# A hardware loop over the middle tiles on VectorE, and waits moved to other engines

## The chip, the core and the metric

The kernel runs on one core of a Trainium2 chip. Five engines work side by side, each through its own list of instructions: TensorE, VectorE, ScalarE, GpSimd (POOL) and SyncE (SP). They meet through semaphores, which are counters that an instruction can raise, lower or wait for. Sixteen DMA engines move data between the chip's large memory (DRAM) and the on-chip memory of 128 partitions. The metric is the time of one execution on the device, in microseconds; given is the median of ten runs.

## What is computed

The input is a float32 array of 8 x 64 x 256 x 256. In each plane of 256 x 256, every 8 x 8 window has its own maximum subtracted from it. The output has the size of the input.

```python
def reference(x):
    B, C, H, W = x.shape
    pH, pW = 8, 8
    oH, oW = H // pH, W // pW
    x_r = x.reshape(B, C, oH, pH, oW, pW)
    pooled = x_r.max(axis=(3, 5))
    upsampled = np.repeat(np.repeat(pooled, pH, axis=2), pW, axis=3)
    return (x - upsampled).astype(np.float32)
```

Input and output are 134.2 MB each. Every byte is read once and written once.

## The kernel before

Eight lines of a plane, 2,048 values, form a "row": it holds 32 whole windows. There are 16,384 rows, 128 for each of 128 partitions. A tile is 4 rows in each partition, so 512 rows or 4 MB, and there are 32 tiles. Six tile buffers (slots) lie on the chip, and tile i uses slot i mod 6. The subtraction works in place, so a slot holds a tile from its load until its store has landed.

Nothing schedules this kernel. It is written for four hands, and each engine takes its own instructions in the order of the loop over the tiles in line 46:

- SyncE issues the loads (L62). Before it loads into a used slot, it waits until the slot's last store has landed (L57, semaphore `stored[slot]`). DMAs raise their semaphore by 16.
- VectorE waits for the load (L75), takes the maximum of each window with one reduce for the whole tile (L76), waits until that reduce has written its result (L87, semaphore `reduced`), and subtracts, with one instruction for each row (L89). The last subtraction raises `ready` (L95).
- ScalarE waits for `ready` (L97) and issues the store (L98). It computes nothing.
- TensorE and GpSimd have no part in it.

The waits of lines 75 and 87 don't become instructions of their own: each is carried by the reduce or the subtraction after it. The semaphore values grow through the kernel, so each of the 32 tiles has its own instructions, with its own numbers in them. VectorE's list has 174 instructions.

Two tiles are cut finer (line 11). The first is loaded in two DMAs of 2 rows and stored in two. The last is loaded whole, and reduced, subtracted and stored in pieces of 2, 1 and 1 rows. At the end SyncE waits for the stores of all six slots (L103).

Of the kernel before, what the change touches and what calls it, by code (L numbers as in the profile page):

```python
# [1 line left out]

# [4 lines left out]

F32 = mybir.dt.float32
ROW = 2048

TILES = [([2, 2], [2, 2])] + [([4], [4])] * 30 + [([4], [2, 1, 1])]
SLOTS = 6
LOAD_SEMS = 10


@with_exitstack
def kernel(
    ctx: ExitStack,
    tc: tile.TileContext,
    x: bass.AP,  # L20
    out: bass.AP,
):
    nc = tc.nc
    P = nc.NUM_PARTITIONS
    B, C, H, W = x.shape
    pH = pW = 8
    oW = W // pW

    x_rows = x.rearrange("b c (oh ph) w -> (b c oh) (ph w)", ph=pH)
    out_rows = out.rearrange("b c (oh ph) w -> (b c oh) (ph w)", ph=pH)  # L30
    assert sum(sum(loads) for loads, _ in TILES) * P == x_rows.shape[0]
    size = max(sum(loads) for loads, _ in TILES)

    data = ctx.enter_context(tc.tile_pool(name="data", bufs=1))
    dats = [data.tile([P, size * ROW], F32, name=f"dat{i}") for i in range(SLOTS)]
    tops = [data.tile([P, size * oW], F32, name=f"tops{i}") for i in range(SLOTS)]
    loaded = [tc.alloc_semaphore(f"loaded{i}") for i in range(LOAD_SEMS)]
    stored = [tc.alloc_semaphore(f"stored{i}") for i in range(SLOTS)]
    reduced = tc.alloc_semaphore("reduced")
    ready = tc.alloc_semaphore("ready")  # L40

    with tc.tile_critical(no_gpsimd_drain=True):  # L42
        at = 0
        n_loads = n_reduced = n_ready = 0
        n_stored = [0] * SLOTS
        for i, (loads, stores) in enumerate(TILES):
            slot = i % SLOTS
            dat, top = dats[slot], tops[slot]

            rows = sum(loads)  # L50
            src = x_rows[at : at + P * rows].rearrange("(p r) d -> p (r d)", r=rows)
            dst = out_rows[at : at + P * rows].rearrange("(p r) d -> p (r d)", r=rows)
            at += P * rows


            if n_stored[slot]:
                nc.sync.wait_ge(stored[slot], 16 * n_stored[slot])  # L57
            lo = 0
            ends = {}
            for R in loads:  # L60
                part = slice(lo * ROW, (lo + R) * ROW)
                nc.sync.dma_start(out=dat[:, part], in_=src[:, part]).then_inc(  # L62
                    loaded[n_loads % LOAD_SEMS], 16
                )
                ends[lo] = (loaded[n_loads % LOAD_SEMS], 16 * (n_loads // LOAD_SEMS + 1))
                n_loads += 1
                lo += R

            lo = 0
            for R in stores:  # L70
                part = slice(lo * ROW, (lo + R) * ROW)
                wins = dat[:, part].rearrange("p (r ph ow pw) -> p r ph ow pw", r=R, ph=pH, ow=oW)
                maxs = top[:, lo * oW : (lo + R) * oW].rearrange("p (r ow) -> p r ow", r=R)
                if lo in ends:
                    nc.vector.wait_ge(*ends[lo])  # L75
                nc.vector.tensor_reduce(  # L76
                    out=maxs if R > 1 else maxs[:, 0],
                    in_=(
                        wins.rearrange("p r ph ow pw -> p r ow ph pw")
                        if R > 1  # L80
                        else wins[:, 0].rearrange("p ph ow pw -> p ow ph pw")
                    ),
                    axis=mybir.AxisListType.XY,
                    op=mybir.AluOpType.max,
                ).then_inc(reduced, 1)
                n_reduced += 1
                nc.vector.wait_ge(reduced, n_reduced)  # L87
                for r in range(R):
                    sub = nc.vector.tensor_tensor(  # L89
                        out=wins[:, r],  # L90
                        in0=wins[:, r],
                        in1=maxs[:, r].unsqueeze(1).unsqueeze(3).to_broadcast([P, pH, oW, pW]),
                        op=mybir.AluOpType.subtract,
                    )
                sub.then_inc(ready, 1)  # L95
                n_ready += 1
                nc.scalar.wait_ge(ready, n_ready)  # L97
                nc.scalar.dma_start(out=dst[:, part], in_=dat[:, part]).then_inc(stored[slot], 16)  # L98
                n_stored[slot] += 1
                lo += R  # L100

        for slot in range(SLOTS):
            nc.sync.wait_ge(stored[slot], 16 * n_stored[slot])  # L103


# [1 line left out]
_INS = ['x']  # L107
_OUTS = [((8, 64, 256, 256), 'float32')]


# [23 lines left out]
```

## Time and profile before

| | |
|---|---|
| median of 10 runs | 627.85 us (627.73 to 628.08) |
| the profiled execution | 627.9 us |
| its span, from the first to the last instruction of the program | 626.1 us |
| one reduce of a whole tile, 30 times | 8.685 us |
| one subtraction of one row, 128 times | 2.286 us |
| load of 4 MB, issue to landing (median) | 62.5 us |
| store of 4 MB, issue to landing (median) | 36.0 us |

The span is what the trace covers; 1.8 us of the execution lie around it. Busy time counts only instructions that compute. The time from issue to landing contains the time in which a transfer stands behind others in its queue: a load of 4 MB has mostly other loads in front of it.

The queues of the trace are called q1 (the loads that SyncE issues), q10 (the stores that ScalarE issues) and q14 (instructions[...]). All of them share the 16 DMA engines.

### The profile page before, as it was taken

The numbers are of one execution on the slowest core, as the hardware profiler recorded it, in microseconds if no ns is written. First come the engines' busy times: TensorE is split into PE (matmuls) and PEld (weight loads), VectorE is DVE, ScalarE is ACT, GpSimd is POOL, SyncE is SP. The second block draws the span as 40 slices with busy tenths as digits, with TensorE's granted clock in tenths as the row PEclk, the third lists the DMA queues.
The fourth block names the chain that finished last, engine by engine and source line by source line (L and its number), as shares of the span: only waits on it lengthen the run. The fifth ranks groups of instructions, "written<-read, shape, count | busy, mean of one in ns | idle before, by whom it ended". The sixth has DMA issues, their size and how long they took to land.

```text
span 626.1 us, 286 instructions
## 1 busy us (share of the span) xinstructions
DVE 562.6 (90%) x163; POOL 0.2 (0%) x4
## 2 busy tenths in 40 slices
DVE  4999999998898888988889888899888998888983
POOL 0000000000000000000000000000000000000000
DMA  8999999999999999999999999999999999999998
GB/s 368 402 431 440 435 435 435 431 433 427 430 431 427 435 435 435 433 435 435 435 435 435 435 429 433 425 435 427 431 435 435 433 435 435 435 435 435 435 429 343
DMA packets 9793, 268.45 MB, mean 429 GB/s; under 512 B 1088, under 2 KB 1088, under 8 KB 1088
## 3 DMA queue, kind: packets, MB, share of 16 engines
q1 hardware_dynamic: 4752, 134.22, 49.9%
q10 hardware_dynamic: 5040, 134.22, 49.7%
q14 instruction: 1, 0.01, 0.0%
HBM read 134.22 MB, written 134.22 MB: 429 GB/s over the span
## 4 chain that ended last, share of the span: by engine, by line
DVE 90%; another core or an unknown queue 7%; DMA 1%; issue 0%; SPq 0%
DVE dat L89 46%; DVE tops L76 44%; DMA dat<-in_x_dram 1%; SPq L129 0%; SPq L42 0%
## 5 line engine op out<-in xcount | busy, mean ns | idle before, releaser
L76 DVE TENSOR_REDUCE tops<-dat 128x128 f32<-128x8192 f32 (+2 forms) x35 | 278.3, 7953 | 52.3 <-DMA dat<-in_x_dram 52.3
L89 DVE TENSOR_TENSOR dat<-dat,tops 128x2048 f32<-128x2048 f32 x128 | 285.0, 2286 | 1.2
L118 POOL MEMSET const-bfloat16-1.0<- 128x1 bf16 x1 | 0.1, 102 | 0.0
L118 POOL MEMSET const-uint8-127<- 128x1 uint8 x1 | 0.1, 102 | 0.0
L118 POOL MEMSET const-float32-0.0<- 128x1 f32 x1 | 0.1, 99 | 0.2 <-issue 0.2
L118 POOL MEMSET const-float32-1.0<- 128x1 f32 x1 | 0.1, 99 | 0.0
## 6 DMA issues: line engine op xcount, KB each, us to landing
dat<-in_x_dram SPq DMA_DIRECT2D x31, 4096.0 KB, 62.5
out_dram<-dat ACTq DMA_DIRECT2D x30, 4096.0 KB, 36.0
out_dram<-dat ACTq DMA_DIRECT2D x3, 2048.0 KB, 19.6
dat<-in_x_dram SPq DMA_DIRECT2D x2, 2048.0 KB, 9.7
out_dram<-dat ACTq DMA_DIRECT2D x2, 1024.0 KB, 9.7
```

Of the source, the lines that this page charges most:

```text
L76: nc.vector.tensor_reduce(out=maxs if R > 1 else maxs[:, 0], in_=(wins.rearrange("p r ph ow pw -> p r ow ph pw") if R > 1 else wins[:, 0]. ...
L89: sub = nc.vector.tensor_tensor(out=wins[:, r], in0=wins[:, r], in1=maxs[:, r].unsqueeze(1).unsqueeze(3).to_broadcast([P, pH, oW, pW]), op ...
L118: nc = _bacc.Bacc("TRN2", target_bir_lowering=False, num_devices=1)
```

## The change

The work on the data is the same: the same tiles, the same reduces and subtractions, one load and one store for each middle tile. What differs is how it is put to the engines.

- VectorE's thirty middle tiles are a loop that the engine itself runs: five turns of an outer loop, six of an inner one over the slots, with one tile as the body (after, L139 to L146). Its list has 55 instructions, 17 of them in the inner loop. Addresses in the body are worked out from the loop's counter, by register instructions in front of the reduce and of the second, third and fourth subtraction.
- Since the body is the same for each tile, it can't wait for growing values. VectorE waits for 1 and lowers the semaphore by 1 (`take`, L73). These waits are instructions of their own, for `reduced` as for the loads.
- Loads raise one semaphore for each slot. TensorE waits for them in the order of the tiles and raises one common semaphore, `filled`, by 1 for each (L116 to L120). VectorE takes from `filled`.
- The six slots are one buffer, `ring`, and the results of the reduces one buffer, `tops`. Tile 0 uses slot 5, tile 1 slot 0, and so on.
- The first tile is loaded, worked on and stored in pieces of 1, 1 and 2 rows. The last is as before.
- The stores of the last six tiles raise one semaphore, `final`, and ScalarE waits for it behind its last store (L133). SyncE has no wait at the end.

```diff
-TILES = [([2, 2], [2, 2])] + [([4], [4])] * 30 + [([4], [2, 1, 1])]
+HEAD = [1, 1, 2]
+SIZE = 4
+ROUNDS = 5
+TAIL = [2, 1, 1]
 SLOTS = 6
-LOAD_SEMS = 10
...
-    dats = [data.tile([P, size * ROW], F32, name=f"dat{i}") for i in range(SLOTS)]
-    tops = [data.tile([P, size * oW], F32, name=f"tops{i}") for i in range(SLOTS)]
-    loaded = [tc.alloc_semaphore(f"loaded{i}") for i in range(LOAD_SEMS)]
+    ring = data.tile([P, SLOTS * SIZE * ROW], F32, name="ring")
+    tops = data.tile([P, SLOTS * SIZE * oW], F32, name="tops")
+    first = [tc.alloc_semaphore(f"first{i}") for i in range(len(HEAD))]
+    loaded = [tc.alloc_semaphore(f"loaded{i}") for i in range(SLOTS)]
     stored = [tc.alloc_semaphore(f"stored{i}") for i in range(SLOTS)]
+    final = tc.alloc_semaphore("final")
+    filled = tc.alloc_semaphore("filled")
     reduced = tc.alloc_semaphore("reduced")
     ready = tc.alloc_semaphore("ready")
...
+    def take(sem, n):
+        nc.vector.wait_ge(sem, n).then_inc(sem, -n)
+
+    def pool_and_subtract(part, top, R):
+        wins = part.rearrange("p (r ph ow pw) -> p r ph ow pw", r=R, ph=pH, ow=oW)
+        maxs = top.rearrange("p (r ow) -> p r ow", r=R)
+        nc.vector.tensor_reduce(
...
+        ).then_inc(reduced, 1)
+        take(reduced, 1)
+        for r in range(R):
+            sub = nc.vector.tensor_tensor(
...
+            )
+        sub.then_inc(ready, 1)
...
+        landed = [0] * SLOTS
+        for i in range(len(sizes)):
+            slot = slot_of(i)
+            if landed[slot]:
+                nc.sync.wait_ge(stored[slot], 16 * landed[slot])
+            for k, (lo, R) in enumerate(cuts(HEAD if i == 0 else [sizes[i]])):
+                part = slice(lo * ROW, (lo + R) * ROW)
+                nc.sync.dma_start(out=sbuf(i, lo, R), in_=dram(x_rows, i)[:, part]).then_inc(
+                    first[k] if i == 0 else loaded[slot], 16
+                )
+                landed[slot] += 1
+
+        for k in range(len(HEAD)):
+            nc.tensor.wait_ge(first[k], 16).then_inc(filled, 1)
+        for i in range(1, len(sizes)):
+            turn = (i - 1) // SLOTS + 1
+            nc.tensor.wait_ge(loaded[slot_of(i)], 16 * turn).then_inc(filled, 1)
+
+        done = n_final = 0
+        for i in range(len(sizes)):
+            for lo, R in cuts(HEAD if i == 0 else TAIL if i == last else [SIZE]):
+                part = slice(lo * ROW, (lo + R) * ROW)
+                done += 1
+                nc.scalar.wait_ge(ready, done)
+                nc.scalar.dma_start(out=dram(out_rows, i)[:, part], in_=sbuf(i, lo, R)).then_inc(
+                    stored[slot_of(i)] if i + SLOTS <= last else final, 16
+                )
+                n_final += i + SLOTS > last
+        nc.scalar.wait_ge(final, 16 * n_final)
...
-        for slot in range(SLOTS):
-            nc.sync.wait_ge(stored[slot], 16 * n_stored[slot])
+        for lo, R in cuts(HEAD):
+            take(filled, 1)
+            pool_and_subtract(sbuf(0, lo, R), top(0, lo, R), R)
+        with nc.vector.Fori(0, ROUNDS):
+            with nc.vector.Fori(0, SLOTS) as slot:
+                take(filled, 1)
+                pool_and_subtract(
+                    ring[:, bass.ds(slot * (SIZE * ROW), SIZE * ROW)],
+                    tops[:, bass.ds(slot * (SIZE * oW), SIZE * oW)],
+                    SIZE,
+                )
+        take(filled, 1)
+        for lo, R in cuts(TAIL):
+            pool_and_subtract(sbuf(last, lo, R), top(last, lo, R), R)
```

## The prediction, made before the changed kernel was run

> **What bounds the kernel now.** I read the page first, sections 1 to 3, for which resource is full; then the waits, for what VectorE lacks; then windows cut where the DMA rate changes; then the timeline of a repeating stretch and of the end.
>
> ```profile
> span 626.1 us, 286 instructions
> ...
> DVE 562.6 (90%) x163; POOL 0.2 (0%) x4
> ...
> DMA  8999999999999999999999999999999999999998
> ...
> q1 hardware_dynamic: 4752, 134.22, 49.9%
> q10 hardware_dynamic: 5040, 134.22, 49.7%
> q14 instruction: 1, 0.01, 0.0%
> ```
>
> VectorE (DVE) is busy for 90% of the span, but the two data queues fill the 16 DMA engines for 99.6% (49.9 + 49.7). The last line is one transfer that carries instructions and not data; it matters below.
>
> ```profile
> DVE tops L76 <- DMA dat<-in_x_dram: 52.3, 26, 8.4
> ```
>
> In the waits, VectorE waits for loads alone: 8.4 us at the start, and 43.9 us over 25 later waits, 1.76 each.
>
> ```profile
> 1.90:4.00 2.10, 0.00 (x0) 0.00 (x0) 1.00 1.05 328
> 4.00:18.00 14.00, 9.54 (x4) 0.00 (x0) 1.00 1.02 438
> 18.00:24.00 6.00, 5.96 (x3) 0.00 (x0) 1.00 0.96 339
> 24.00:131.00 107.00, 106.79 (x32) 0.00 (x0) 1.00 1.01 434
> 131.00:598.00 467.00, 422.41 (x121) 0.00 (x0) 1.00 1.00 433
> 598.00:620.00 22.00, 17.89 (x7) 0.00 (x0) 1.00 1.00 430
> ```
>
> The windows (stretch, VectorE busy, POOL busy, clock, DMA share, GB/s) show the DMA at 430 to 438 GB/s from 4 us to 620, but for 18 to 24 us. So the time is 268.4 MB at that rate, plus the ends. Up to 131 us VectorE is behind (busy for 106.8 of 107 us) and the DMA is full all the same. After it VectorE is ahead and waits for each tile.
>
> ```profile
> 141.62 8.90 DVE L89 TENSOR_TENSOR dat<-dat,tops 128x2048 f32<-128x2048 f32 x4
> 152.25 8.69 DVE L76 TENSOR_REDUCE tops<-dat 128x128 f32<-128x8192 f32 x1 [1.73 <-DMA dat<-in_x_dram]
> 160.97 8.90 DVE L89 TENSOR_TENSOR dat<-dat,tops 128x2048 f32<-128x2048 f32 x4
> 172.29 8.69 DVE L76 TENSOR_REDUCE tops<-dat 128x128 f32<-128x8192 f32 x1 [2.42 <-DMA dat<-in_x_dram]
> ```
>
> The timeline gives the slack: a tile costs VectorE 8.69 + 8.90 + 0.03 = 17.62 us, and one comes every 19.34 us (the chain of waits has reduces at 191.62, 210.96, 230.30). That is 1.72 us of room a tile. One interval is 0.7 longer: 152.25 to 172.29 is 20.04. The packet records say why. The instruction transfer starts at 164.87 us: 8,192 bytes, 309 ns on one engine, and the packet beside it took 1,747 ns where every other 32,768-byte one of that stretch took 1,213. That engine lost 309 + 534 = 843 ns. Each engine moves its own 16.8 MB, so it stays behind: linked end to end, 15 engines finish their last packet between 623.50 and 623.92 us, and one at 624.46. The kernel waits for that one. Then come the landing of the last store (about 624.8) and the closing barrier, to 626.1. VectorE is long done:
>
> ```profile
> 613.83 2.29 DVE L89 TENSOR_TENSOR dat<-dat,tops 128x2048 f32<-128x2048 f32 x1
> ```
>
> Its last store is issued at 616.2 us and lands 8.6 us later, behind other stores: the tail of VectorE has cover as well.
>
> [...] in the trace VectorE's one branch took 47 ns.
>
> **The change, part by part.** The sum is made on the profiled execution: 627.9 us, of which 626.1 are span and 1.8 lie around it.
>
> 1. *VectorE's stream shrinks from 174 instructions to 55, the loop being 17 of them.* Before, the fetch began while VectorE worked on the second subtraction of the ninth tile, about the 48th instruction of its stream[...]: the border lies some 50 to 60 instructions in. In the new stream the loop is roughly numbers 18 to 37, short of it, and the end of the stream only touches it after the last tile. So I take the fetch as gone from the data phase. Worth: the last engine to finish moves from 624.46 to the next one's 623.92, **-0.54 us**. Bounds: 0 if the fetch only moves, -0.84 if the other engines come out level.
>
> 2. *What the loop adds to a VectorE tile.* Two separate waits in place of waits carried by the reduce and the first subtraction, four register instructions for addresses, a counter and a branch, and every sixth tile the outer ones. Three of the address steps and the loop's end come while a subtraction of 2.29 us runs, and hide behind it. Exposed are: TensorE's pass-on of the load (its semaphore instruction took 51 ns), VectorE's semaphore instruction twice (21 ns each in the trace), one address step (not shown; I take a branch's 47 ns[...]), and two restarts, where the trace of before has 0.02 to 0.03 us each[...]. [...] I take 0.2 us a time. Sum 0.05 + 0.04 + 0.05 + 2 x 0.2 = 0.54 us, **0.5**; the bounds are 0.15 (restarts as now) and 1.5. Tile 17.62 + 0.5 = 18.1, under 19.34: **0** on the path. The cover is the 1.72 us. If it is gone, the excess counts in each of thirty tiles. In the first stretch VectorE catches up at 19.34 - 18.1 = 1.2 us a tile where it did at 1.7, so its first wait comes near 185 us and not at 131; the DMA has loads and stores queued throughout, so that costs nothing.
>
> 3. *Head cut 1, 1, 2 in place of 2, 2, with a third load issue (0.33 us) and a third store.* The first row is in after about half of the data time: a 2 MB load landed at 8.4 us, a 1 MB one should at about 6, and the first store goes out at 6 + 2.28 + 2.29, near 11, not at 17.4. The DMA is full from 2 us, so an earlier store only changes the mix. Cost: a 16,384-byte packet takes 611 ns and two of 8,192 take 618. Each engine has eight such in the split load and eight in the split store: 16 x 7 = 0.11, with two more semaphore packets at 9 ns **+0.13 us**. Unknown is the slow spell at 18 to 24 us: (433 - 339) x 6 us is 0.56 MB, 1.3 us, around the first store (issued at 17.41, first packet at 21.24). It should come with any first store, only sooner: **0**, bounds -1.0 (less of it with a smaller store) and +0.6 (a second spell, for a second small store).
>
> 4. *End.* SyncE's waits on six counters and its pass to the others become one wait on ScalarE, behind its last store; nothing is queued after it but the barrier. Before, SyncE went from 624.8 (its branch) to 625.2 through its own semaphore, drains of VectorE and ScalarE, and back; now ScalarE's drain and one hop stay: **-0.2 us**, bounds -0.3 and 0.
>
> 5. *Tail.* Three reduces and their waits are as before but with separate waits: three restarts and one pass-on, about 0.7 us later than 616.2. The last store of 1 MB needs 2.4 us and starts when the others drain, near 622. Even after the 3.8 us that the first store took to its first packet, 616.9 leaves room: **0**. TensorE's 33 waits have an engine to themselves; SyncE's loads stand in the same order and wait for the same stores.
>
> Sum: 627.9 - 0.54 + 0.13 - 0.2 = 627.3. The profiled execution lies 0.05 above the median of 627.85, so the median comes out at 627.2 to 627.3; I say **627.3 us**.
>
> **Rivals.**
>
> *The turn of the loop outgrows its slack* (slower). Place: from the end of the last subtraction to the next reduce, and from a reduce to its first subtraction. With an extra of x a tile, VectorE starts tile 1 near 24.5 and needs 30 x (17.62 + x), then 18 for the last tile and about 4.3 for the last store to land. That passes the DMA's 624.5 from x = 1.64 us on. At x = 2.5[...] it is 24.5 + 603.6 + 18 + 4.3 + 1.3 = 651.7 of span, **653 us**. For it: nothing in the trace shows an address taken from a register, nor a backward branch. Against: x would have to be three times my sum[...]. Chance 0.17.
>
> *The fetch doesn't go away* but falls into the tail or to TensorE's longer stream: items 3 and 4 alone, **627.8 us**. For it: the border is known only to some ten instructions. Chance 0.2, within 0.2% either way.
>
> *The slow spell around the first store shrinks with it:* 627.3 - 1.0 = **626.3 us**. For it: a smaller first store has fewer first packets. Against: the loads slowed before any store packet began, which looks like a fixed price. Chance 0.13.
>
> **How the numbers follow.** The forecast, with the fetch gone and nothing else moved, has 0.5. 0.2% is 1.26 us, about what a measurement of this kernel can tell from no change. Forecast and second rival lie inside it, but for 0.02 on either side for errors that add up. The third rival is faster, but for 0.02 that it ends just inside: 0.11 + 0.02 = 0.13 faster. The first rival and such errors are slower: 0.17 + 0.02 = 0.19. The rest, 0.68, is the same. The likeliest case's own range is 626.6 to 628.2 (bounds of items 1, 3 and 4 taken together, not all at their worst). For 8 in 10 it reaches down to the third rival, 626.1, and up to 629.2, where a small overrun of the slack (x near 1.7) would end; the rest of the first rival is left out.
>
> **What would show it.** No instruction transfer inside the span, and no 0.7 us slip of one tile; the last packets of the 16 engines level. VectorE's wait before a reduce down from 1.73 to about 1.2, with periods of 19.34 as before; a gap of 0.1 to 0.3 us between a reduce and its first subtraction. The slow spell as large as before, but at 12 to 18 us. Wrong if VectorE stops waiting for loads after 200 us, if the period exceeds 19.34, or if many instruction transfers appear.

## The result, and the profile after

The changed kernel takes 643.76 us (median of 8 runs, 642.43 to 644.70) against 627.82 for the kernel before: a ratio of 1.0253, 95% interval 1.0244 to 1.0262. It is 16 us slower; the forecast was 627.3 us, with a range up to 629.2.

The page of the changed kernel, with the lines that answer to those shown of before:

```profile
span 641.9 us, 619 instructions
...
DVE 562.8 (88%) x164; POOL 0.2 (0%) x4
...
DMA  9999999999999999999999999999999999999995
...
q1 hardware_dynamic: 4896, 134.22, 50.2%
q10 hardware_dynamic: 5184, 134.22, 48.6%
```

VectorE computes for as long as before, 562.8 us. The instruction queue q14 has no line any more: no instruction transfer falls into the span. The two data queues fill the DMA engines almost as before (98.8% of the span), with the same 268.4 MB, for 15.8 us longer. So the same bytes take longer. The windows of the changed kernel say where (stretch, length, VectorE busy, POOL busy, clock, DMA share, GB/s):

```profile
12.00:18.00 6.00, 5.85 (x3) 0.00 (x0) 1.00 0.97 407
18.00:24.00 6.00, 5.85 (x3) 0.00 (x0) 1.00 1.00 430
24.00:131.00 107.00, 105.03 (x31) 0.00 (x0) 1.00 1.01 432
131.00:300.00 169.00, 150.43 (x43) 0.00 (x0) 1.00 1.00 424
300.00:500.00 200.00, 176.03 (x51) 0.00 (x0) 1.00 1.00 423
500.00:598.00 98.00, 85.41 (x25) 0.00 (x0) 1.00 1.00 422
```

From 131 us on the rate is 422 to 424 GB/s where it was 433, at a share of 1.00: the engines are not idle, their packets take longer. The wait of VectorE in the changed kernel is named after the semaphore instruction that stands in front of the reduce (L75):

```profile
DVE tops L81 <- DVEq L75: 61.0, 26, 5.9
```

It waits 61.0 us where it waited 52.3. VectorE is further from being the bound than before, not nearer. The timeline of the changed kernel, first while VectorE is behind, and then in the steady stretch:

```profile
60.63 8.68 DVE L81 TENSOR_REDUCE tops<-ring  x1
...
69.46 8.90 DVE L93 TENSOR_TENSOR ring<-ring,tops  x4
78.28 8.68 DVE L81 TENSOR_REDUCE tops<-ring  x1
```

```profile
229.93 8.69 DVE L81 TENSOR_REDUCE tops<-ring  x1 [1.98 <-DVEq L75]
238.76 8.90 DVE L93 TENSOR_TENSOR ring<-ring,tops  x4
250.16 8.69 DVE L81 TENSOR_REDUCE tops<-ring  x1 [2.50 <-DVEq L75]
258.99 8.90 DVE L93 TENSOR_TENSOR ring<-ring,tops  x4
269.81 8.69 DVE L81 TENSOR_REDUCE tops<-ring  x1 [1.92 <-DVEq L75]
```

The kernel before, while VectorE is behind:

```profile
26.15 8.68 DVE L76 TENSOR_REDUCE tops<-dat 128x128 f32<-128x8192 f32 x1
34.86 8.90 DVE L89 TENSOR_TENSOR dat<-dat,tops 128x2048 f32<-128x2048 f32 x4
43.68 8.68 DVE L76 TENSOR_REDUCE tops<-dat 128x128 f32<-128x8192 f32 x1
```

While VectorE is behind, a tile takes 78.28 - 60.63 = 17.65 us; before, it took 43.68 - 26.15 = 17.53. The loop costs about 0.1 us a tile. In the steady stretch tiles come after 20.23 and 19.65 us, on average 19.9 where it was 19.34, and the idle time in front of the reduce has grown and not shrunk.

The packet records of the DMA carry the rest. In the kernel before, of 7,536 packets of 32 KB after 40 us, 7,534 took 1,213 ns to the nanosecond, and one was over 1,243, the line that I draw for a slow packet. In the changed kernel 528 load packets and 130 store packets were over it, up to 2.5 us; with the smaller delays all packets together took 180 us too long, or 11.2 us for each of the 16 engines. They are not shared out evenly: linked end to end, the engines finish between 632.45 and 640.49 us, on average at 635.3. Before, the average was 623.75 and the last 624.46. So the last packet moved by 16.0 us: 11.5 for the average engine, and 4.5 because the engines drifted apart.

### The profile page after: what moved, and what is told of

It is laid out like the page before. It is cut to its first block, busy times and chain, and to the rows that moved or that the text cites. A ratio compares the mean times of both kernels' runs of the same rounds, so it can differ in the third digit from the quotient of the medians.

```text
span 641.9 us, 619 instructions
## 1 busy us (share of the span) xinstructions
DVE 562.8 (88%) x164; POOL 0.2 (0%) x4
## 5 line engine op out<-in xcount | busy, mean ns | idle before, releaser
L81 DVE TENSOR_REDUCE tops<-ring (+2 forms) x36 | 278.5, 7736 | 61.0 <-DVEq L75 61.0
L93 DVE TENSOR_TENSOR ring<-ring,tops (+1 forms) x128 | 285.1, 2286 | 5.3 <-DVEq L75 0.2
## 6 DMA issues: line engine op xcount, KB each, us to landing
ring<-in_x_dram SPq DMA_DIRECT2D x1, 2048.0 KB, 11.2
```

The lines of the kernel that those rows point to most:

```text
L81: nc.vector.tensor_reduce(out=maxs if R > 1 else maxs[:, 0], in_=(wins.rearrange("p r ph ow pw -> p r ow ph pw") if R > 1 else wins[:, 0]. ...
L93: sub = nc.vector.tensor_tensor(out=wins[:, r], in0=wins[:, r], in1=maxs[:, r].unsqueeze(1).unsqueeze(3).to_broadcast([P, pH, oW, pW]), op ...
```

## The experiments

**Which part of the change.** At the start there were three theories. P: the new cut of the first tile brings loads and stores into another phase. V: VectorE's loop or waits, or TensorE's pass-on, disturb. M: the single buffer, or the shift of the slots by one. Four runs undo or do one part each. Here and below a kernel ran once, unless a number of runs is given.

The kernel before, with the new cut alone (`a_head`):

```diff
-TILES = [([2, 2], [2, 2])] + [([4], [4])] * 30 + [([4], [2, 1, 1])]
+TILES = [([1, 1, 2], [1, 1, 2])] + [([4], [4])] * 30 + [([4], [2, 1, 1])]
```

> The kernel before, with the first tile cut 1, 1, 2 for loads and stores, and nothing else changed. Theory P (phase): the 16 us come from DMA packets that run slower because the earlier first store and the level start of the 16 engines put load and store boundaries of the tiles into another phase; then this kernel is slow too, 636 to 646 us, with hundreds of load packets over 1,213 ns. Theory V (VectorE's separate waits, register steps, loop or TensorE's pass-on disturb): this kernel stays at 627.5 to 628.2 us, with no slow load packets after 30 us. Theory M (one ring buffer, or the slots shifted by one): 627.5 to 628.2 us.

The changed kernel with the old cut (`b_head22`):

```diff
-HEAD = [1, 1, 2]
+HEAD = [2, 2]
```

> The changed kernel with the first tile cut 2, 2 again. Theory P: fast again, 626.5 to 628.5 us. Theory V and theory M: still slow, 638 to 646 us.

The changed kernel with the loop written out (`c_unrolled`):

```diff
-        with nc.vector.Fori(0, ROUNDS):
-            with nc.vector.Fori(0, SLOTS) as slot:
-                take(filled, 1)
-                pool_and_subtract(
...
+        for i in range(1, last):
+            take(filled, 1)
+            pool_and_subtract(sbuf(i, 0, SIZE), top(i, 0, SIZE), SIZE)
```

> The changed kernel with VectorE's loop written out (30 tiles with fixed addresses, the separate waits and TensorE's pass-on kept). Theory P: still slow, 638 to 646 us. Theory V, if it is the loop and its register instructions: 627 to 628.5 us; if it is the separate waits or TensorE: still slow. Theory M: still slow.

The kernel before with shifted slots (`d_slot`):

```diff
-            slot = i % SLOTS
+            slot = (i - 1) % SLOTS
```

> The kernel before, with tile i in slot (i - 1) mod 6, so tile 0 in slot 5. Theory M, if it is the shift of the slots: 636 to 646 us. Theories P and V: 627.5 to 628.2 us.

Measured: `a_head` 672.25 us, `b_head22` 627.43, `c_unrolled` 643.80, `d_slot` 627.82, with the kernel before at 627.70 on the same chip. The cut alone is slower still than the whole change; the change without the cut is not slow; the loop and the slots make no difference. V and M are out. The rate row of the page of `a_head` shows something that the changed kernel hasn't got:

```profile
GB/s 371 420 430 435 434 426 422 422 438 424 419 428 420 428 424 426 422 424 411 434 409 436 424 426 422 422 432 420 422 403 426 389 409 395 389 407 172 233 363 157
```

Some thirty slices are like those of the changed kernel; then the rate is below 410 in most of them, and at 172 and 233 near the end. One engine had fallen a whole tile behind the others by 304 us: its part of a load landed some 20 us after the first one's. VectorE needs the slowest engine's part of a load, and a slot is free only when the slowest engine has stored its part, so the other 15 had to wait: from 600 to 640 us half of all engine time was idle. That an engine falls so far behind was not foreseen; my upper end for this run was 646.

**What it is about the cut.** In each queue an engine works through tile after tile: a load tile ends, the next begins, and the same for stores; both queues mostly take turns, packet by packet (before, linked end to end, 5,881 of 6,815 packets of 32 KB from 40 to 560 us follow one of the other queue). The records show the ends, as the small packets that raise the semaphore (4 bytes, 9 ns). The time from the end of a load tile to the next end of a store tile (first engine to get there) stays the same through a run once both queues are never empty (in `a_head` and `l_head4_spare` until the drift had grown to about a tile). It is 15.8 us in the kernel before, 16.6 in `b_head22`, and 2.5 us in the changed kernel, `a_head` and `c_unrolled`. Theory P then says: a store tile that ends so soon after a load tile slows the packets. Its rival: the small early pieces leave the engines in some bad state.

An added load of 1 MB moves the load queue against the store queue without touching any piece of the first tile. In the changed kernel (`f_after_spare1`):

```diff
+EXTRA = 1
...
+            if i == 0:
+                nc.sync.dma_start(out=spare, in_=dram(x_rows, 0)[:, : EXTRA * ROW]).then_inc(spared, 16)
...
```

> The changed kernel, with one more load of 1 MB (one row in each partition, into a buffer that nothing reads) behind the loads of the first tile. It moves the stream of loads back by two 32 KB packets on each engine against the stream of stores. In the changed kernel a tile of the stores ended 2.4 us after a tile of the loads; here it should end about 2.5 us before one, near the 3.6 us of the kernel before. Phase theory (the distance between the two borders decides): the slow packets go, 628 to 632 us, faster than the changed kernel although it moves 1 MB, 2.4 us, more. Theory of the small pieces (1 MB loads and stores at the start set the engines level or leave some other trace): slow still, 642 to 648 us.

In the kernel before, twice 1.4 MB, one behind each load of the first tile (`g_before_spare`):

```diff
+EXTRA = 2816
...
                 n_loads += 1
                 lo += R
+                if i == 0:
+                    if n_loads == 2:
+                        nc.sync.wait_ge(spared, 16)
+                    nc.sync.dma_start(out=spare, in_=src[:, :EXTRA]).then_inc(spared, 16)
...
```

> The kernel before, with two more loads of 1.4 MB each (into a buffer that nothing reads), one behind each of the first two loads. They move the loads back by 5.5 packets, so that a tile of the stores should end 1 to 4 us after a tile of the loads, as in the changed kernel. Bytes alone: 627.8 + 6.7 = 634.5 us. Phase theory: slow packets appear, 642 to 670 us. Theory of the small pieces: 634 to 636 us, no slow load packets after 40 us.

The new cut for the loads alone (`h_loads112`):

```diff
-TILES = [([2, 2], [2, 2])] + [([4], [4])] * 30 + [([4], [2, 1, 1])]
+TILES = [([1, 1, 2], [2, 2])] + [([4], [4])] * 30 + [([4], [2, 1, 1])]
...
```

> The kernel before with the first tile loaded in 1, 1, 2 rows but reduced and stored in 2, 2. The first store goes out at 17.4 us as before, so the borders stand as before. Phase theory: 627.6 to 628.4 us. If the small loads themselves are to blame (the engines start more level): 636 us or more.

And the changed kernel with other DRAM addresses for the loads, at the same times, so that it computes on other input rows (`e_addr`):

```diff
...
-                nc.sync.dma_start(out=sbuf(i, lo, R), in_=dram(x_rows, i)[:, part]).then_inc(
+                nc.sync.dma_start(out=sbuf(i, lo, R), in_=dram(x_rows, i, 16 if 0 < i < last else 0)[:, part]).then_inc(
```

> The changed kernel with the loads of the thirty middle tiles taken 16 rows (128 KB, four packets) further on in the input; the output is then not the reference's. Timing and order of every transfer stay the same; only the DRAM addresses that are read while others are written move. If packets slow down because reads and writes meet at DRAM addresses that collide: another time than 643.7, either back to 626 to 630 us or at least 5 us off. If what counts is only where the borders of the transfers stand in the queues: 642 to 645 us again.

Measured: `f_after_spare1` 629.80 us, 14 us faster than the changed kernel though it moves 1 MB more; the distance is 14.6 us. `h_loads112` 627.55 at 15.1 us. `e_addr` 643.78 at 2.5 us: moving the addresses by 128 KB changed nothing (this one shift was tried). `g_before_spare` missed its aim. While stores were still few its distance was 1.8 us, but it settled at 12.1 when the store queue had caught up, and its 634.02 us is what the bytes cost. It is one more fast case at another distance, and no test of a short one.

For the next four I counted packets first (an engine takes load and store packets mostly in turns; most took 309, 611 or 1,213 ns, for 8, 16 or 32 KB), to choose cuts that give wanted distances. The counts, 12, 5, 7 and 2.5 us, came out at 10.6, 4.8, 8.4 and 2.5. The changed kernel with loads of 1, 1, 2 rows, but work and stores in 1 and 3 (`i_work13`):

```diff
+WORK = [1, 3]
...
-            for lo, R in cuts(HEAD if i == 0 else TAIL if i == last else [SIZE]):
+            for lo, R in cuts(WORK if i == 0 else TAIL if i == last else [SIZE]):
...
-        for lo, R in cuts(HEAD):
-            take(filled, 1)
+        for lo, R in cuts(WORK):
+            take(filled, 1 if lo == 0 else 2)
```

> The changed kernel, loads of the first tile 1, 1, 2 as there, but worked on and stored in 1 and 3 rows. The first store of 1 MB leaves at 10.7 us as in the changed kernel; only the two later pieces become one. Counting packets by hand (load and store packets take turns on an engine), a store tile should now end 12 us after a load tile, not 2.5. Phase theory: 626.5 to 628 us, hardly any load packet over 1,243 ns after 40 us. Theory of the small pieces (an early first store of 1 MB leaves the engines in a bad state): 638 us or more.

The kernel before with three other first tiles, the last one with an added load (`j_head4`, `k_stores112`, `l_head4_spare`):

```diff
+TILES = [([4], [4])] + [([4], [4])] * 30 + [([4], [2, 1, 1])]
```

```diff
+TILES = [([2, 2], [1, 1, 2])] + [([4], [4])] * 30 + [([4], [2, 1, 1])]
```

```diff
+TILES = [([4], [4])] + [([4], [4])] * 30 + [([4], [2, 1, 1])]
...
+EXTRA = 1024
...
+            if i == 0:
+                nc.sync.dma_start(out=spare, in_=src[:, :EXTRA]).then_inc(spared, 16)
...
```

> The kernel before with the first tile loaded, worked on and stored whole. By the same count a store tile ends about 5 us after a load tile, twice the distance of the changed kernel. Phase theory: slow if 5 us is still near enough, 632 to 645 us, else 627 to 628.5; this run says how wide the bad zone is. Theory of the small pieces: 627 to 629 us, as there are none.

> The kernel before with the first tile loaded in 2, 2 and worked on and stored in 1, 1, 2. By the count a store tile ends about 7 us after a load tile. Phase theory: 626.5 to 629 us, if 7 us is outside the bad zone. Theory of the small pieces, if it is the stores: 636 us or more.

> The kernel with a whole first tile, and one more load of 0.5 MB (into a buffer that nothing reads) behind it. Bytes alone add 1.2 us to the whole first tile's time. By the count a store tile ends about 2.5 us after a load tile, as in the changed kernel. Phase theory: slow, 640 us or more, though it has the loop-free VectorE list and no small store at all. Theory of the small pieces: 628 to 630 us.

Measured: `i_work13` 627.37 us (12 runs; ratio 0.9992, interval 0.9983 to 1.0001), `k_stores112` 627.47, `j_head4` 632.16, `l_head4_spare` 654.60. The first has the small early store and is not slow. The last has no small store, no early store and no loop, and is slow. The same window (stretch, length, VectorE busy, POOL busy, clock, DMA share, GB/s) of `i_work13`, then of `l_head4_spare`:

```profile
131.00:598.00 467.00, 423.82 (x122) 0.00 (x0) 1.00 1.00 433
```

```profile
131.00:598.00 467.00, 406.49 (x117) 0.00 (x0) 1.00 1.00 422
```

The first has the rate of the kernel before, the second that of the changed kernel, at a DMA share of 1.00 in both. All runs, by distance; a slow packet is one of 32 KB after 40 us that took over 1,243 ns, the drift is between the first and the last engine at the last load but one:

| kernel | distance, us | slow load, store packets | drift, us | time, us |
|---|---|---|---|---|
| before | 15.8 | 1, 0 | 2.2 | 627.82 |
| d_slot | 15.5 | 1, 0 | 1.9 | 627.82 |
| h_loads112 | 15.1 | 1, 0 | 1.5 | 627.55 |
| b_timed (as b_head22) | 16.1 | 1, 0 | 2.0 | 627.28 |
| f_after_spare1 (1 MB more) | 14.6 | 5, 1 | 2.8 | 629.80 |
| g_before_spare (2.9 MB more) | 12.1 | 12, 0 | 0.9 | 634.02 |
| i_work13 | 10.6 | 0, 1 | 1.7 | 627.37 |
| k_stores112 | 8.4 | 21, 0 | 2.0 | 627.47 |
| j_head4 | 4.8 | 79, 32 | 6.7 | 632.16 |
| after | 2.5 | 528, 130 | 11.0 | 643.76 |
| c_unrolled | 2.5 | 534, 120 | 11.9 | 643.80 |
| e_addr | 2.5 | 552, 107 | 11.4 | 643.78 |
| m_late_loads | 2.5 | 520, 103 | 10.2 | 642.24 |
| n_two_stores | 2.4 | 588, 75 | 6.8 | 639.46 |
| l_head4_spare (0.5 MB more) | 2.5 | 348, 798 | 19.5 | 654.60 |
| a_head | 2.5 | 442, 408 | 21.0 | 672.25 |

Whatever else differs, the distance tells which kernels lose time. From 8 us up a few packets are slow and the time doesn't show it; at 4.8 us it costs 4 us; at 2.5 us 12 to 45.

It is the order of the two ends that counts, and not their nearness alone. At the full rate a load tile ends every 19.36 us, so a distance of 15.8 us also says that the store tile ends 3.6 us before the next load tile. In `b_head22` (16.6) it ends 2.7 us before it, on most single engines 2.4 us, one packet of each queue. In the changed kernel it ends 2.5 us after the load tile, on most engines 2.4. The ends are as near in one as in the other, and `b_head22` has one slow packet where the changed kernel has 658. What the runs show to be slow is a store tile that ends 2.5 to 4.8 us after a load tile; 8.4 to 16.6 us after it was harmless. What lies between 4.8 and 8.4 us and beyond 16.6 was not run, and below 2.5 us no run stayed throughout.

**Where the slow packets stand.** In the changed kernel, linking each engine's packets and counting the excess over 1,213 ns of load packets by their place between two ends of a store tile on the same engine (60 to 560 us, the 357 stretches in which the link finds the eight store packets of a tile; where engines run level it can swap two of them):

```
store packets since the end of a store tile   0     1     2    3    4    5    6    7    8
excess of load packets, us                    31.3  31.6  3.2  1.4  0.2  0.1  0.2  0.0  71.4
```

134 of 139 us fall on the load packet just before the end of a store tile and on the two just after it. Counted from the end of the load tile, nearly all falls on the first three packets of the next load tile. In the middle of a tile the packets run at full pace, at the same distance. So in the changed kernel it isn't that loads and stores stand at like places of their tiles all the time; it is the passage of the two ends. The two slowest runs add something else: store packets carry 91 of 183 us of excess in `a_head` and 135 of 215 in `l_head4_spare` (10 of 163 in the changed kernel), in `l_head4_spare` spread over the whole tile. Why is open.

**What happens at the passage.** Two more of its companions were to be moved away. In the changed kernel a new load is issued just after the store's end, and a third store is under way for some 5 us of each tile. `m_late_loads` issues the load later, `n_two_stores` holds the third store back:

```diff
+                nc.sync.wait_ge(ready, i)
```

```diff
+                if 2 <= i <= 27:
+                    turns = (i - 2 - 1) // SLOTS + 1
+                    nc.scalar.wait_ge(stored[slot_of(i - 2)], 16 * (turns + (len(HEAD) if slot_of(i - 2) == slot_of(0) else 0)))
```

> The changed kernel; SyncE waits, beside the landed store, until VectorE has finished the tile three before the one to be loaded. In the changed kernel's steady stretch this moves the issue of each load about 15 us away from the end of a store tile, into the middle of the tiles; order and addresses of the transfers stay, and a store tile should still end 2.5 us after a load tile. If the packets slow down because a new load is set up just when both queues change tiles: 626 to 629 us. If it is enough that both queues end a tile within 2.5 us: 640 to 646 us again.

> The changed kernel; ScalarE issues a store only when the store two tiles earlier has landed, so never three at once. In the changed kernel a third store is under way for about 5 us of each tile; in the kernel before never more than two. If the third store in the queue is what slows the load packets: 626 to 629 us. If it is enough that both queues end a tile within 2.5 us: 640 to 648 us again.

Measured: 642.24 and 639.46 us, both still slow, with 520 and 588 slow load packets. `m_late_loads` doesn't settle its question: from 200 to 540 us its issues fall between 1.5 us before and 5 us after the first engine's end of the next store tile, and not in the middle of a tile. `n_two_stores` settles both: never more than two stores are under way (150 to 500 us), and of its 375 slow load packets from 200 to 540 us, 355 start more than 10 us after the last issue of any load or store. Neither an issue close by nor the third store is needed. The 4 us of `n_two_stores` go with a smaller drift, 6.8 us for 11.0. What holds a packet up when a store tile ends just after a load tile is not in the trace, and stays open.

**The rest of the change, by itself.** `b_timed` is the kernel of `b_head22` again, with an interval:

> The changed kernel with the first tile cut 2, 2 (as in b_head22), timed with an interval: what the loop, the waits, TensorE's pass-on and ScalarE's last wait are worth without the new cut. The prediction's sum without its part 3 is -0.54 - 0.2 = -0.74 us, 627.1 us. Phase theory with loop costs hidden: 627.0 to 627.6 us, ratio 0.9988 to 0.9997. If the loop costs something on the path: 627.9 us or more.

Measured: 627.28 us (21 runs) against 627.77: ratio 0.9995, interval 0.9988 to 1.0001. The median is 0.5 us lower, but the interval holds 1. Its timeline:

```profile
229.93 8.69 DVE L81 TENSOR_REDUCE tops<-ring  x1 [1.63 <-DVEq L75]
238.77 8.90 DVE L93 TENSOR_TENSOR ring<-ring,tops  x4
249.30 8.69 DVE L81 TENSOR_REDUCE tops<-ring  x1 [1.63 <-DVEq L75]
```

The period is 249.30 - 229.93 = 19.37 us, as before, and the wait is 1.63 us where it was 1.73: the loop's 0.1 us is taken out of VectorE's idle time. `b_timed` and `i_work13` have the lowest medians of all runs, 0.5 us under the kernel before beside them; neither is shown to beat it.

## Why the prediction was wrong

The step that failed is part 3, in the sentence "The DMA is full from 2 us, so an earlier store only changes the mix". I priced the new cut by its packets, +0.13 us, with bounds of -1.0 and +0.6. It cost 16.3: 643.76 less the 627.4 that the same kernel took without it. In place of a harmless mix, the cut moved the end of a store tile from 15.8 to 2.5 us after the end of a load tile, and there the packets lost 11.2 us on each engine, and the engines drifted apart for 4.5 more. The early store by itself does no harm: `i_work13` has it, at a distance of 10.6 us, and takes 627.37. The mix was taken to be harmless, because the kernel before showed one rate over 600 us. But it showed that rate at one distance only; the profile of before could not say what another would do, and my bounds came from the slow spell at the start instead of from that ignorance. The records did hold a hint: thousands of packets of exactly 1,213 ns can be read as two queues in a fixed step, and the change moves the step.

By the other steps:

- *Part 1, the fetch.* It is gone from the span in the changed kernel, in `b_timed` and in `i_work13`, as said. Its worth of 0.54 us isn't shown by itself. In `b_head22` two engines that had lost time otherwise end at 624.2 us, so the last packet came 0.25 us earlier there. The last packets of the 16 engines were to come out level: in `b_head22` they lie within 1.0 us, in the changed kernel they spread over 8. That the transfer at 164.87 us was VectorE's, and that the border lay some 50 to 60 instructions in, were my estimates; no record names the engine. In the changed kernel the trace has thirty-five branch instructions at the ends of the loop (L139, L140), of 50 to 63 ns each, and no instruction transfer.
- *Part 2, the loop.* Right, and dearer in my sum than on the chip: 0.5 us expected, 0.1 measured. The 0.2 us for a restart was my guess. One address step takes 99 ns on VectorE (L81), and a restart after a reduce 0.15 us (0.03 before). The first rival, the loop that outgrows its slack, lay on the right side of zero for the wrong reason. Its 2.5 us a tile was my guess as well, and no run shows it. Of its signs, the longer period is there; but "VectorE stops waiting for loads" is the opposite of what the trace shows, and that tells the two causes apart. The slower side had 0.19 of the chances, nearly all of it for this mechanism.
- *Part 3, the slow spell.* Its place moved to 12 to 18 us as said. Its size did not stay: (433 - 407) x 6 us is 0.16 MB or 0.4 us, not 1.3. That is the third rival's mechanism, but no run is 1 us faster for it: `i_work13` has the small early store, 429 GB/s from 18 to 24 us, and one slow packet, and takes 627.37.
- *Part 4, the end.* The last packet ends at 640.49 and the span at 641.93, 1.44 us; before it was 1.66. That is the 0.2 us.
- *Part 5, the tail.* VectorE ends its last subtraction at 629.04 us and the last packet 11.4 us later: covered.

Together parts 1, 2, 4 and 5 gave 627.1 to 627.2 for the change without the cut; measured are 627.28 and 627.43.

## What to carry to other kernels

Here a load queue and a store queue fill the DMA together (99.6% of the span before, 98.8% after), and the profile of one version shows one phase between them: 15.8 us before, 2.5 after. The sizes and times of the first transfers set it for most of the run. Where two queues fill the DMA like this, treat an edit to the first pieces as a change to that phase, and look at when tiles end in each queue, and in which order: here a store tile did no harm when it ended 8.4 to 16.6 us after a load tile, of a period of 19.4, and did harm at 2.5 to 4.8. That is measured for this size of tile and packet alone. A cut priced at 0.13 us cost 16 over the run, and a change with several parts is best timed with the head alone undone.

## What the runs showed that I had not expected

- The same bytes in the same sizes ran at 433 or at 423 GB/s, at a DMA share of 1.00 both times; the busy row doesn't tell the two apart, the packet times do (1,213 ns against up to 2.5 us).
- The loss grows through the slots: the engines drift apart (2 us before, 11 in the changed kernel, 21 in `a_head`), and when the drift reaches a whole tile, all engines wait for the slowest. So the same cut cost 45 us in `a_head` (one run) and 16 in the changed kernel, with the loop or without. Why the drift grows faster in one than in the other was not tried.
- A register address costs VectorE little: 99 ns for the step in front of the reduce, and nothing seen on the subtractions, which take 2,286 ns with a register address and 2,290 with a fixed one.
